# A decoder layer with expert retrieval on one core: priority for weight splits, a routing table read in pairs, up rows in longer runs

## The chip, the cores and the metric

The kernel runs on one core of a Trainium2 chip. A core has engines with an instruction queue each: TensorE (PE, matmuls; PEld is its weight load), VectorE (DVE), ScalarE (ACT), GpSimd (POOL) and SyncE (SP, which here only issues DMAs). Every engine executes its own instructions in a fixed order and waits by semaphores for the others. The metric is the time of one execution in device microseconds; lower is better.

## The reference

One layer over T = 1024 tokens of width D = 1024, all in float32: a token mixer (gated convolution plus dilated attention), then a feed-forward part that retrieves experts:

```
h = x + mixer(rms_norm(x))
u = rms_norm(h)
q = (u @ w_query).reshape(T, 8, 2, 128)        # 8 heads, two half keys
# product keys: 16 best of 128 per half, 16 best of 16*16 sums
idx, gates = ...                               # 8*16 = 128 of 16384 experts per token
a   = gelu(einsum('cd,ced->ce', u, down[idx]))
h   = h + einsum('ce,ced->cd', gates * a, up[idx])
out = rms_norm(h)
```

`down` and `up` are 16384 x 1024 each (64 MB each), and a token uses 128 rows of either.

## The kernel before

**Two ways to the experts.** Tiles of 128 tokens are treated in two ways. For tiles 0, 2 and 3 (the *side*, `experts()`) every token fetches its own rows: for each of the 128 picks POOL issues a gather of 128 rows of `down`, 512 KB (L873), DVE forms the dot product (L875), and after all of them the same with rows of `up` (L889, accumulated into `acc` on DVE, L891). That is 512 products with `down` (tile 1 takes part in these) and 384 accumulations with `up`, into four gather buffers. Tokens 512 to 1023, and the second half of tile 1's work, go through *all* experts densely, on PE.

**The dense way** has two stages. In the *hidden stage* `hidden(q)` takes four chunks of 128 experts: `weights()` (L160 to L168) loads a 512 KB chunk of `down_t`, 24 matmuls of 512 columns form its hidden values, ACT applies the gelu into `ga`. The first `STORED` = 27 of 32 groups are written to memory (`a_d`) and fetched again later; `HOLD` = 4 stay on the core; the group that is left is computed within the up stage. Beside it a builder makes the routing table `g_d` (which token uses which expert with which gate) from one-hot matrices, with matmuls (L975), copies (L977) and writes (L981). In the *up stage* each of 32 steps reads its piece of the table (`gg`, L985; `gx`, L996, for tile 1), multiplies the hidden values by it (L990) and does 120 matmuls with rows of `up` (L1063), which are summed in `held` banks, or in `psu` banks with an addition into `rest` (L1089). The last step adds the sums to `h1b` (L1093), normalizes and writes out (L855, L856).

**Float32 by halves.** Each float32 operand is split in two: `hi` is a rounding copy on ACT (L165 for weights, L181 elsewhere), `lo` the residue on DVE (L167, L182). A product then takes three matmuls, L176 (hi, hi), L177 and L178 with one `lo` each (`mm3`). For weights there are four load buffers (`RAWS`) and two pairs of `hi`/`lo` (`HILO`).

**What sets the order.** A list scheduler places the instructions of all engines by priority, which is the order in which they were written unless a block raises it. The program text interleaves the main work with the side by `yield`ed costs; the resulting order on each engine is fixed when the kernel is built. Table reads, weights and up rows share SP's queue, in issue order.

Of the kernel before, what the change touches and what calls it, by code (L numbers as in the profile page):

```python
# [8 lines left out]
F32 = mybir.dt.float32  # L9
# [4 lines left out]
ALU = mybir.AluOpType  # L14
# [3 lines left out]
P = 128  # L18
T = 1024
TH = 512  # L20
# [11 lines left out]
TC = 32  # L32
NB = 4
# [1 line left out]
PACE_D = 2.0  # L35
PACE_C = 2.2
RATE_G = 0.8
STORED = 27
HOLD = 4
RAWS = 4  # L40
HILO = 2
# [22 lines left out]

@with_exitstack
def hybrid_layer(ctx, tc, x, xT, pos, rotc, norm_mix, w_proj, w_v, conv_w, w_conv_out, w_attn_out,
                 gate_bias, w_out, norm_ffn, w_query, sub_keys, down, down_t, up, final_norm, out):
    nc = tc.nc
    V, S, G, PE = nc.vector, nc.scalar, nc.gpsimd, nc.tensor
    SIDE = getattr(nc, QUEUE)  # L70
# [90 lines left out]
    def weights(src, n=8):  # L161
        raw = wp.tile([P, n, D // n], F32, tag="raw", bufs=RAWS, name="raw")
        nc.sync.dma_start(raw, src)
        hi = wp.tile([P, n, D // n], F32R, tag="hi", bufs=HILO, name="hi")
        S.copy(hi, raw)  # L165
        lo = wp.tile([P, n, D // n], F32R, tag="lo", bufs=HILO, name="lo")
        V.tensor_tensor(lo, raw, hi.bitcast(F32), op=ALU.subtract)  # L167
        return hi, lo  # L168

    def bank(b, name):  # L170
# [729 lines left out]
    def dense():  # L900
# [47 lines left out]
        def build(srcs, c0):  # L948
# [5 lines left out]
                for c in range(c0, c0 + P // TC):  # L954
# [25 lines left out]
                    for w in range(4):  # L980
                        nc.sync.dma_start(g_d[c, :, 32 * w:32 * w + 32], stg[w])  # L981

        def weigh(q):
            gg = m8.tile([P, TH // TC, NB, TC], F32, tag="big", name="gg")
            nc.sync.dma_start(gg, g_d[:TH // TC, :, NB * q:NB * q + NB].rearrange("c j i t -> j c i t"))  # L985
            ga = gas.pop(q)
            hh, hl = bigr("hh"), bigr("hl")
            for ii in range(NB):
                v = ga[:, ii].rearrange("p (c t) -> p c t", t=TC)
                V.tensor_tensor(v, v, gg[:, :, ii], op=ALU.mult)  # L990
                split(hh[:, ii], hl[:, ii], ga[:, ii])
            parts = [(hh[:, :, tt * P:tt * P + P], hl[:, :, tt * P:tt * P + P]) for tt in range(4)]
            for k in range(len(XT)):
                gx = up_p.tile([P, P // TC, NB, TC], F32, tag="gx", bufs=GXB, name="gx")
                c0 = (TH + k * P) // TC
                nc.sync.dma_start(gx, g_d[c0:c0 + P // TC, :, NB * q:NB * q + NB].rearrange("c j i t -> j c i t"))  # L996
                xh = up_p.tile([P, NB, P], F32R, tag="xh", bufs=XHB, name="xh")
                xl = up_p.tile([P, NB, P], F32R, tag="xl", bufs=XHB, name="xl")
                view = [t.rearrange("p i (c t) -> p c i t", t=TC) for t in (xh, xl)]
                S.copy(view[0], gx)  # L1000
                V.tensor_tensor(view[1], gx, view[0].bitcast(F32), op=ALU.subtract)
                parts.append((xh, xl))
            return parts
# [30 lines left out]
        for n_q, q in enumerate(order):  # L1034
# [22 lines left out]
            for n in range(2):  # L1057
                uu = []
                whole = [bigr("uh_end"), bigr("ul_end")] if end and n else None
                for ii in range(0, NB, 2):  # L1060
                    raw = wp.tile([P, 2, TH], F32, tag="raw", bufs=RAWS, name="rawu")
                    r0 = (NB * q + ii) * P
                    nc.sync.dma_start(raw, up[r0:r0 + 2 * P, n * TH:n * TH + TH].rearrange("(a p) d -> p a d", a=2))  # L1063
                    if whole:
                        uh, ul = (t[:, ii:ii + 2] for t in whole)
                    else:
                        uh = up_p.tile([P, 2, TH], F32R, tag="uu", bufs=UPS, name="uh")
                        ul = up_p.tile([P, 2, TH], F32R, tag="uu", bufs=UPS, name="ul")
                    split(uh, ul, raw)
                    uu.append((uh, ul))  # L1070
# [105 lines left out]
```

## Time and profile before

| quantity | value |
|---|---|
| median of 3 runs | 3423.3 us (3423.22 to 3426.72) |
| profiled execution, its own time | 3433.88 us |
| its span, first to last instruction | 3432.1 us |
| PE / DVE / ACT / POOL busy | 95% / 80% / 43% / 35% of the span |
| mean granted TensorE clock | 0.984 of full speed |
| DMA | 948.08 MB in 364307 packets, 276 GB/s on average |

The span is what the rows below are cut from; 1.8 us of the profiled execution lie outside of it. Stages by the trace: mixer and query work until 1609 us (the gathers start at about 600 us), the hidden stage until 2491 us, the up stage until the end.

### The profile page before, as it was taken

The numbers are of one execution on the slowest core, as the hardware profiler recorded it, in microseconds if no ns is written. First come the engines' busy times: TensorE is split into PE (matmuls) and PEld (weight loads), VectorE is DVE, ScalarE is ACT, GpSimd is POOL, SyncE is SP. The second block draws the span as 40 slices with busy tenths as digits, with TensorE's granted clock in tenths as the row PEclk, the third lists the DMA queues.
The fourth block names the chain that finished last, engine by engine and source line by source line (L and its number), as shares of the span: only waits on it lengthen the run. The fifth ranks groups of instructions, "written<-read, shape, count | busy, mean of one in ns | idle before, by whom it ended". The sixth has DMA issues, their size and how long they took to land.

```text
span 3432.1 us, 47074 instructions
## 1 busy us (share of the span) xinstructions
PE 3274.4 (95%) x15923; PEld 2685.0 (78%) x15923; DVE 2760.1 (80%) x5646; ACT 1461.7 (43%) x3271; POOL 1190.2 (35%) x944
## 2 busy tenths in 40 slices
PE   7999999999989999988999989999999999999998
PEld 6787888887767777767777878888877878787787
DVE  4333355689999889988999999998887878888887
ACT  3544444443334353333226777787632222222222
POOL 0000000014543345555434443464544334444342
PEclk9999999999989999989999999999999999999999
DMA  4233335668888678988889898999989989999895
GB/s 129 77 119 110 103 127 191 244 230 305 302 279 276 227 260 307 342 316 292 315 316 328 329 330 334 344 340 336 348 301 336 334 316 338 326 340 333 309 350 208
DMA packets 364307, 948.08 MB, mean 276 GB/s; under 512 B 33952, under 2 KB 127648, under 8 KB 356640
## 3 DMA queue, kind: packets, MB, share of 16 engines
q1 hardware_dynamic: 232016, 465.27, 38.9%
q0 software_dynamic: 132048, 479.78, 38.8%
q8 instruction: 126, 2.06, 0.2%
q14 instruction: 117, 0.96, 0.1%
HBM read 843.15 MB, written 95.49 MB: 273 GB/s over the span
## 4 chain that ended last, share of the span: by engine, by line
PE 32%; DVE 20%; DMA 14%; issue 11%; POOL 5%; ACT 1%; SPq 0%; DVEq 0%; POOLq 0%; ACTq 0%
DVE row L875 6%; PE ps L178 6%; PE ps L176 6%; PE ps L177 6%; DMA row<-in_down,idx 5%; DMA rowu<-in_up,idx 4%; DMA gg<-g_d 4%; DVE lo L167 3%; POOL row L873 3%; POOL rowu L889 2%; PE held L177 2%; PE held L178 2%; PE held L176 2%; DVE acc L891 1%; PE psg L975 1%
## 5 line engine op out<-in xcount | busy, mean ns | idle before, releaser
L873 POOL DMA_INDIRECT row<-in_down,idx x512 | 640.9, 1252 | 885.2 <-DVE a L875 465.6
L889 POOL DMA_INDIRECT rowu<-in_up,idx x384 | 525.8, 1369 | 621.1 <-DVE acc L891 499.0
L165 ACT CAST hi<-raw 128x1024 fp32r<-128x1024 f32 x368 | 387.6, 1053 | 746.0 <-PE ps L177 541.1
L875 DVE CUSTOM_DVE_ANT_0 row<-row,ut 128x1024 f32<-128x1024 f32 x512 | 618.8, 1215 | 79.2 <-DMA row<-in_down,idx 74.0
L167 DVE TENSOR_TENSOR lo<-raw,hi 128x1024 fp32r<-128x1024 f32 x368 | 448.1, 1218 | 247.9 <-ACT hi L165 238.6
L178 PE MATMUL ps<-vhi,lo 128*128 128x512 f32 (+1 forms) x1408 | 535.4, 382 | 33.5 <-DVE lo L167 33.4
L176 PE MATMUL ps<-vhi,hi 128*128 128x512 f32 (+1 forms) x1408 | 530.6, 377 | 10.8 <-ACT hi L165 6.7
L891 DVE SCALAR_TENSOR_TENSOR acc<-rowu,a,acc 128x1024 f32<-128x1024 f32 x384 | 491.2, 1279 | 59.7 <-DMA rowu<-in_up,idx 57.3
L177 PE MATMUL ps<-vlo,hi 128*128 128x512 f32 (+1 forms) x1408 | 528.9, 376 | 0.0
L178 PE MATMUL ps<-uhi,lo 128*128 128x512 f32 x1024 | 409.1, 400 | 4.2 <-DVE lo L167 4.2
L176 PE MATMUL ps<-uhi,hi 128*128 128x512 f32 x1024 | 407.6, 399 | 5.7 <-ACT uhi L181 3.1
L177 PE MATMUL ps<-ulo,hi 128*128 128x512 f32 x1024 | 409.1, 400 | 0.5 <-DVE ulo L182 0.5
L178 PEld LDWEIGHTS ps<-vhi,lo 128*128 128x128 f32 x1408 | 269.1, 191 | 87.4 <-DVE lo L167 44.4
L176 PEld LDWEIGHTS ps<-vhi,hi 128*128 128x128 f32 x1408 | 269.7, 192 | 58.9 <-ACT hi L165 10.9
L177 PEld LDWEIGHTS ps<-vlo,hi 128*128 128x128 f32 x1408 | 269.1, 191 | 45.1
L177 PE MATMUL held<-ul,hh 128*128 128x512 f32 x624 | 247.0, 396 | 11.1 <-DVE ul L182 10.9
L178 PE MATMUL held<-uh,hl 128*128 128x512 f32 x624 | 244.0, 392 | 2.5 <-DVE hl L182 2.5
L176 PEld LDWEIGHTS ps<-uhi,hi 128*128 128x128 f32 x1024 | 194.1, 190 | 52.1 <-ACT uhi L181 5.2
L176 PE MATMUL held<-uh,hh 128*128 128x512 f32 x624 | 233.3, 393 | 0.0
L178 PEld LDWEIGHTS ps<-uhi,lo 128*128 128x128 f32 x1024 | 194.3, 190 | 47.9 <-DVE lo L167 6.4
L177 PEld LDWEIGHTS ps<-ulo,hi 128*128 128x128 f32 x1024 | 194.1, 190 | 45.1 <-issue 3.0
L181 ACT CAST hh<-ga 128x512 fp32r<-128x512 f32 x128 | 71.4, 618 | 353.0 <-DVE ga L990 348.9
(347 smaller groups left out, 5947.8 us busy)
## 6 DMA issues: line engine op xcount, KB each, us to landing
raw<-in_w_proj SPq DMA_DIRECT2D x128, 512.0 KB
raw<-in_down_t SPq DMA_DIRECT2D x128, 512.0 KB
rawu<-in_up SPq DMA_DIRECT2D x128, 512.0 KB
g_d<-stg SPq DMA_DIRECT2D x80, 512.0 KB
gg<-g_d SPq DMA_DIRECT2D x32, 1024.0 KB
a_d<-ga SPq DMA_DIRECT2D x27, 1024.0 KB
ga<-a_d SPq DMA_DIRECT2D x27, 1024.0 KB
raw<-in_w_query SPq DMA_DIRECT2D x48, 512.0 KB
```

What stands on the lines that cost most here:

```text
L165: S.copy(hi, raw)
L167: V.tensor_tensor(lo, raw, hi.bitcast(F32), op=ALU.subtract)
L176: PE.matmul(ps, l[0], r[0], start=first, stop=False)
L177: PE.matmul(ps, l[0], r[1], start=False, stop=False)
L178: PE.matmul(ps, l[1], r[0], start=False, stop=last)
L181: S.copy(hi, src)
L873: G.indirect_dma_start(out=row, out_offset=None, in_=down, in_offset=bass.IndirectOffsetOnAxis(ap=idx[:, e:e + 1], axis=0))
L875: V.tensor_tensor_reduce(out=row, in0=row, in1=ut, scale=1.0, scalar=0.0, op0=ALU.mult, op1=ALU.add, accum_out=a[:, e:e + 1])
L889: G.indirect_dma_start(out=row, out_offset=None, in_=up, in_offset=bass.IndirectOffsetOnAxis(ap=idx[:, e:e + 1], axis=0))
L891: V.scalar_tensor_tensor(acc, row, a[:, e:e + 1], acc, op0=ALU.mult, op1=ALU.add)
L975: PE.matmul(ps[:, t], ob[:, t], oa[:, t], start=True, stop=True)
```

## The change

Four edits. In `weights()` the cast and the residue are written under the scheduler's highest priority. `weigh(q)` reads the routing table for two steps in one pair of transfers: two tiles of 1 MB, each half of the tokens for eight chunks, whose runs in memory are 1 KB instead of 512 bytes, kept for both steps. It also works on half of the tokens and all four chunks at once, so the step has two products, casts and residues of 128x4x256 in place of four of 128x512. The rows of `up` come from a second copy of `up`, arranged on the host, in which one transfer's partition reads one run of 4 KB instead of two of 2 KB. `STORED` is 28, so the group that was computed within the up stage moves to the hidden stage, with one more 1 MB store and fetch.

```diff
-STORED = 27
+STORED = 28
...
         hi = wp.tile([P, n, D // n], F32R, tag="hi", bufs=HILO, name="hi")
-        S.copy(hi, raw)
         lo = wp.tile([P, n, D // n], F32R, tag="lo", bufs=HILO, name="lo")
-        V.tensor_tensor(lo, raw, hi.bitcast(F32), op=ALU.subtract)
+        with tc.high_priority():
+            S.copy(hi, raw)
+            V.tensor_tensor(lo, raw, hi.bitcast(F32), op=ALU.subtract)
...
+        pairs = {}
+
         def weigh(q):
-            gg = m8.tile([P, TH // TC, NB, TC], F32, tag="big", name="gg")
-            nc.sync.dma_start(gg, g_d[:TH // TC, :, NB * q:NB * q + NB].rearrange("c j i t -> j c i t"))
+
+            c2 = TH // TC // 2
+            if q // 2 not in pairs:
+                both = []
+                for half in range(2):
+                    gg = m8.tile([P, c2, 2 * NB, TC], F32, tag="big", name="gg")
+                    i0 = 2 * NB * (q // 2)
+                    nc.sync.dma_start(gg, g_d[c2 * half:c2 * half + c2, :, i0:i0 + 2 * NB].rearrange("c j i t -> j c i t"))
+                    both.append(gg)
+                pairs[q // 2] = both
+            gg2 = pairs[q // 2]
             ga = gas.pop(q)
             hh, hl = bigr("hh"), bigr("hl")
-            for ii in range(NB):
-                v = ga[:, ii].rearrange("p (c t) -> p c t", t=TC)
-                V.tensor_tensor(v, v, gg[:, :, ii], op=ALU.mult)
-                split(hh[:, ii], hl[:, ii], ga[:, ii])
+            for half in range(2):
+                cols = slice(half * TH // 2, half * TH // 2 + TH // 2)
+                v = ga[:, :, cols]
+                g = gg2[half][:, :, NB * (q % 2):NB * (q % 2) + NB].rearrange("p c i t -> p i c t")
+                V.tensor_tensor(v.rearrange("p i (c t) -> p i c t", t=TC), v.rearrange("p i (c t) -> p i c t", t=TC), g,
+                                op=ALU.mult)
+                split(hh[:, :, cols], hl[:, :, cols], v)
...
-                    r0 = (NB * q + ii) * P
-                    nc.sync.dma_start(raw, up[r0:r0 + 2 * P, n * TH:n * TH + TH].rearrange("(a p) d -> p a d", a=2))
+                    nc.sync.dma_start(raw, up_s[(NB * q + ii) // 2, n])
...
+        "up_s": i["peer_up"][0].reshape(P // 2, 2, P, 2, TH).transpose(0, 3, 2, 1, 4),
```

How the instructions stand now is shown at three places.

**DVE in the hidden stage**, between two weight residues (`lo`, the 262nd and 263rd of 368 by program order) while tile 1's rows of `down` are gathered (L875) and the picks of a dense tile are sorted out (L811, L814). Before:

```order
L167 TENSOR_TENSOR lo<-raw,hi 128x1024
L875 ISA row,a<-row,ut 128x1024
L875 ISA a 128x1
L811 SCALAR_TENSOR_TENSOR wq<-paf,tif 128x256
L814 TENSOR_TENSOR e_15037<-e_15037,wq 128x256
L875 ISA row,a<-row,ut 128x1024
L875 ISA a 128x1
L814 TENSOR_TENSOR other<-other,wq 128x256
L811 SCALAR_TENSOR_TENSOR wq<-paf,tif 128x256
L875 ISA row,a<-row,ut 128x1024
L875 ISA a 128x1
L167 TENSOR_TENSOR lo<-raw,hi 128x1024
```

The same place of the changed kernel:

```order
L168 TENSOR_TENSOR lo<-raw,hi 128x1024
L876 ISA row,a<-row,ut 128x1024
L876 ISA a 128x1
L815 TENSOR_TENSOR e_15037<-e_15037,wq 128x256
L815 TENSOR_TENSOR other<-other,wq 128x256
L876 ISA row,a<-row,ut 128x1024
L876 ISA a 128x1
L812 SCALAR_TENSOR_TENSOR wq<-paf,tif 128x256 x2
L876 ISA row,a<-row,ut 128x1024
L876 ISA a 128x1
L168 TENSOR_TENSOR lo<-raw,hi 128x1024
```

Three gathered rows stand between the two residues in both. Over the whole program the residues up to about the 290th stand behind the same number of gathered rows as before, within one, and behind up to ten fewer small operations; from there on the lead grows, to 13 gathered rows and some tens of smaller operations at the 319th. So the gathered rows reach the up stage later: 17 of the accumulations (L891, now L892) still stand behind the first eviction of the result.

**SP at the switch from the hidden to the up stage**: last writes of the table, up rows (`rawu`), table reads (`gg`, `gx`). Before:

```order
L981 DMA g_d<-stg 128x1024 x4
L1063 DMA rawu<-in_up 128x2x512 x2
L985 DMA gg<-g_d 128x16x128
L996 DMA gx<-g_d 128x4x128 x2
L1063 DMA rawu<-in_up 128x2x512 x4
L996 DMA gx<-g_d 128x4x128
L985 DMA gg<-g_d 128x16x128
L1063 DMA rawu<-in_up 128x2x512 x3
```

After:

```order
L982 DMA g_d<-stg 128x1024 x4
L1077 DMA rawu<-in_up_s 128x1024 x2
L1011 DMA gx<-g_d 128x4x128 x2
L994 DMA gg<-g_d 128x8x256 x2
L1077 DMA rawu<-in_up_s 128x1024 x4
L1011 DMA gx<-g_d 128x4x128
L994 DMA gg<-g_d 128x8x256 x2
L1077 DMA rawu<-in_up_s 128x1024 x4
```

The first table read now stands behind both `gx`, and two transfers of 1 MB stand where one did. On PE 128 matmuls of the hidden stage follow the last one-hot product before the first of the up stage; before there were 106.

**DVE at the end**, around the first evictions of the result (`h1b` plus `held` or `psu`). Before:

```order
L891 SCALAR_TENSOR_TENSOR acc<-rowu,a,acc 128x1024 x2
L1001 TENSOR_TENSOR xl<-gx,xh 128x4x4x32
L200 TENSOR_SCALAR st<-st 128x1
L202 RECIPROCAL st<-st 128x1
L203 TENSOR_TENSOR st<-st 128x1
L204 TENSOR_TENSOR st<-st 128x1
L205 TENSOR_SCALAR st<-st 128x1
L206 TENSOR_TENSOR st<-st 128x1
L855 SCALAR_TENSOR_TENSOR acc<-acc,st,nfin 128x1024
L1093 TENSOR_TENSOR h1b_28853<-h1b_28853,held_22593 128x512
```

After:

```order
L892 SCALAR_TENSOR_TENSOR acc<-rowu,a,acc 128x1024 x2
L1016 TENSOR_TENSOR xl<-gx,xh 128x4x4x32
L892 SCALAR_TENSOR_TENSOR acc<-rowu,a,acc 128x1024 x3
L1107 TENSOR_TENSOR h1b_28664<-h1b_28664,held_22750 128x512
L892 SCALAR_TENSOR_TENSOR acc<-rowu,a,acc 128x1024
L1107 TENSOR_TENSOR h1b_28664<-h1b_28664,psu 128x512
L1107 TENSOR_TENSOR h1b_28665<-h1b_28665,psu 128x512
L892 SCALAR_TENSOR_TENSOR acc<-rowu,a,acc 128x1024
L1107 TENSOR_TENSOR h1b_28664<-h1b_28664,held_22745 128x512
```

The gathered tiles were finished before the first eviction; now their accumulations are spread between and behind the ten evictions, with 17, 16, 16, 15, 12, 11, 10, 8, 7 and 6 still to come at each.

## Rows read from the trace of the kernel before

**Rows 1.** The page of the profile: busy time of each engine (share of the span, number of instructions), and the two large DMA queues with packets, megabytes and the time of their packets as a share of 16 engines' span. q1 carries the transfers that SP issues, q0 the gathers that POOL issues.

```profile
PE 3274.4 (95%) x15923; PEld 2685.0 (78%) x15923; DVE 2760.1 (80%) x5646; ACT 1461.7 (43%) x3271; POOL 1190.2 (35%) x944
...
q1 hardware_dynamic: 232016, 465.27, 38.9%
q0 software_dynamic: 132048, 479.78, 38.8%
```

**Rows 2.** The span cut at the stages' edges: length, busy time of PE, PEld, DVE, ACT and POOL with the number of their instructions, mean granted TensorE clock, DMA share, GB/s. 1609 to 1812 and 1812 to 2491 are the hidden stage (without and with the building of the routing table beside it), 2491 to 3423 the up stage, 2700 to 2800 a piece out of its middle.

```profile
600.00:1300.00 700.00, 663.25 (x3674) 546.50 (x3673) 621.15 (x1794) 296.95 (x579) 242.30 (x217) 0.96 0.79 267
1300.00:1609.00 309.00, 278.72 (x1257) 227.94 (x1255) 270.42 (x431) 103.94 (x194) 164.32 (x125) 0.96 0.89 317
1609.00:1812.00 203.00, 183.53 (x779) 144.64 (x778) 192.82 (x631) 60.94 (x91) 86.40 (x74) 0.99 0.88 310
1812.00:2491.00 679.00, 658.60 (x3499) 562.69 (x3499) 636.97 (x1194) 497.83 (x1559) 316.24 (x222) 0.99 0.91 337
2491.00:3423.00 932.00, 911.41 (x3936) 739.33 (x3936) 766.78 (x1015) 234.34 (x329) 378.99 (x296) 1.00 0.89 319
2700.00:2800.00 100.00, 100.00 (x438) 82.02 (x437) 83.01 (x125) 25.56 (x34) 36.44 (x30) 1.00 0.91 329
```

**Rows 3.** What PE waited for from 600 to 1300 us (columns: total us, times, longest): the two groups of waits for a weight residue. The third row is the same wait in 1300 to 1609.

```profile
PE pv L177 <- DVE lo L167: 8.3, 3, 4.0
...
PE ps L178 <- DVE lo L167: 4.9, 4, 2.2
...
PE ps L178 <- DVE lo L167: 9.1, 6, 3.6
```

**Rows 4.** The same list for 1609 to 1812.

```profile
PE ps L178 <- DVE lo L167: 12.7, 12, 2.7
PE ps L176 <- ACT hi L165: 5.2, 8, 0.9
```

**Rows 5.** The same list for 1812 to 2491.

```profile
PE ps L178 <- DVE lo L167: 9.7, 6, 1.9
PE ps L176 <- ACT hi L165: 1.4, 2, 0.9
```

**Rows 6.** The same list for 2491 to the end.

```profile
PE held L177 <- DVE ul L182: 10.9, 9, 2.4
PE ps L176 <- ACT ga L913: 3.0, 1, 3.0
PE held L178 <- DVE hl L182: 2.5, 1, 2.5
```

**Rows 7.** What DVE waited for from 2491 to the end: a piece of the routing table, and gathered rows of `up`.

```profile
DVE ga L990 <- DMA gg<-g_d: 73.3, 26, 8.4
DVE acc L891 <- DMA rowu<-in_up,idx: 32.7, 30, 4.1
```

**Rows 8.** One stall of the hidden stage in order of time (start, us, engine, line, operation, count, in brackets the idle time before it and what ended it): the cast on ACT, the residue on DVE behind a gathered row, and the matmul on PE.

```profile
1747.17 1.05 ACT L165 CAST hi<-raw 128x1024 fp32r<-128x1024 f32 x1 [3.89 <-PE ps L177]
...
1748.07 1.22 DVE L875 CUSTOM_DVE_ANT_0 row<-row,ut 128x1024 f32<-128x1024 f32 x1 [2.50 <-DMA row<-in_down,idx]
1749.22 1.22 DVE L167 TENSOR_TENSOR lo<-raw,hi 128x1024 fp32r<-128x1024 f32 x1
...
1750.49 0.50 PE L178 MATMUL ps<-vhi,lo 128*128 128x512 f32 x1 [2.68 <-DVE lo L167]
```

**Rows 9.** How long DVE stood at a residue whose cast was not done: 600 to 1300, then 1812 to 2491.

```profile
DVE lo L167 <- ACT hi L165: 36.4, 37, 5.1
DVE lo L167 <- ACT hi L165: 14.4, 11, 3.9
```

**Rows 10.** The change from the hidden to the up stage, in order of time: the last writes of the routing table and its first read as SP issues them, the first product with that read on DVE, and the first matmul of the up stage on PE.

```profile
2465.14 2.54 SPq L981 DMA_DIRECT2D g_d<-stg  x4
...
2480.21 0.37 SPq L985 DMA_DIRECT2D gg<-g_d  x1
...
2490.79 2.49 DVE L990 TENSOR_TENSOR ga<-ga,gg 128x512 f32<-128x512 f32 x4
...
2491.42 0.50 PE L176 MATMUL held<-uh,xh 128*128 128x512 f32 x1 [1.20 <-ACT xh L1000]
```

**Rows 11.** Lines of the page's groups that the change rewrites: count, busy us, mean ns of one, idle time of the engine before them.

```profile
L990 DVE TENSOR_TENSOR ga<-ga,gg 128x512 f32<-128x512 f32 x128 | 80.2, 686 | 73.3 <-DMA gg<-g_d 73.3
...
L182 DVE TENSOR_TENSOR hl<-ga,hh 128x512 fp32r<-128x512 f32 x128 | 81.2, 687 | 1.7 <-PE held L177 1.0 <-ACT hh L181 0.7
...
L182 DVE TENSOR_TENSOR ul<-rawu,uh 128x1024 fp32r<-128x1024 f32 x126 | 153.3, 1217 | 14.5 <-ACT uh L181 5.8 <-issue 4.3 <-PE psu L177 4.1
```

**Rows 12.** The end of the span on DVE: last gathered rows, last operation of the gathered tiles, first eviction of the result, last operation of all.

```profile
3395.20 2.59 DVE L891 SCALAR_TENSOR_TENSOR acc<-rowu,a,acc 128x1024 f32<-128x1024 f32 x2
...
3401.50 1.28 DVE L855 SCALAR_TENSOR_TENSOR acc<-acc,st,nfin 128x1024 f32<-128x1024 f32 x1
3402.70 0.68 DVE L1093 TENSOR_TENSOR h1b<-h1b,held 128x512 f32<-128x512 f32 x1
...
3427.58 1.42 DVE L855 SCALAR_TENSOR_TENSOR h1b<-h1b,sts,nfin 128x512 f32<-128x512 f32 x2
```

**Rows 13.** The pace of gathered rows with little else on DVE: the first and the last of four (two stand between them).

```profile
2467.08 1.29 DVE L891 SCALAR_TENSOR_TENSOR acc<-rowu,a,acc 128x1024 f32<-128x1024 f32 x1 [2.39 <-DMA rowu<-in_up,idx]
...
2475.71 1.28 DVE L891 SCALAR_TENSOR_TENSOR acc<-rowu,a,acc 128x1024 f32<-128x1024 f32 x1 [1.22 <-DMA rowu<-in_up,idx]
```

More of the change, by code (lines that the diff above doesn't have):

```diff
@@ L66, in hybrid_layer @@
 def hybrid_layer(ctx, tc, x, xT, pos, rotc, norm_mix, w_proj, w_v, conv_w, w_conv_out, w_attn_out,
-                 gate_bias, w_out, norm_ffn, w_query, sub_keys, down, down_t, up, final_norm, out):
+                 gate_bias, w_out, norm_ffn, w_query, sub_keys, down, down_t, up, up_s, final_norm, out):
     nc = tc.nc
```

## The prediction

> **What bounds the kernel now.** I read the page's busy line first: PE is busy for 3274.4 us of the 3432.1, DVE for 2760.1, and nothing else comes near [rows 1]. PE is therefore what sets the time, and a change can only win where PE stands or runs slowly; about 158 us of idle time are all there is. Next I cut the span by stages, because DVE's average of 80% hides its peaks [rows 2]. The reader should see two different regimes. In the hidden stage DVE is busy for 192.8 of 203 us and for 637.0 of 679 us, almost as tightly as PE: 10.2 and 42.0 us are left in which any of its work could be late. In the up stage it has 165 us to spare, the middle of the stage runs PE for 100.00 of 100 us, and the number of matmuls there (438 in 100 us) gives 0.228 us for each. Then I asked what PE waited for in each stage. In the hidden stage it is nearly always a weight residue, `lo`, or its cast, `hi` [rows 4, 5]; in the up stage it is the split of up rows and of the weighted hidden values [rows 6]. Last I followed one stall and the end of the span on DVE [rows 8, 12].
>
> The stall shows the mechanism that the change's first edit aims at. The cast was done at about 1748.2. DVE stood for a gathered row (2.50 us), did its product, began the residue at 1749.22, and PE, which had needed it for 2.68 us, went on at 1750.49. So PE's waits are not for DVE's throughput alone: a residue stands in line behind a product whose data come late.
>
> I make the sum on the profiled execution, 3433.9 us with its span of 3432.1. The median of the runs shown is 3423.3, so I carry the differences over to that.
>
> **The change, part by part.**
>
> *Priority of cast and residue.* The two instructions remain the same, 368 each; only their place changes, and it can change only by what stands ahead of them. The rows of the order tell two cases. Up to about the 290th residue the same gathered rows stand ahead, and a few small operations fewer; at the place shown, three rows before and three after. There a late row still blocks the residue. From there to the end of the hidden stage up to 13 rows fewer stand ahead.
> - Up to 1609 us: the waits shown are 8.3, 4.9 and 9.1 us, 22.3 together [rows 3]. With the same rows ahead I take 3 us off. Bounds: 0 and 22.
> - 1609 to 1812: 12.7 + 5.2 = 17.9 us of waits, and a granted clock of 0.99, worth about 2 us over 203 [rows 2, 4]. A few small operations of some 0.4 us leave the way, rows stay. I take 8, a little under half. Bounds: 0 and 20.
> - 1812 to 2491: 9.7 + 1.4 = 11.1 us, and 0.01 of clock over 679 us, 7 us [rows 2, 5]. Here rows do leave the way, so I take all of the waits and none of the clock: 11. Bounds: 0 and 18.
>
> A cast that goes first on ACT costs nothing by itself: ACT had stood for 3.89 us before the one shown, until PE released the `hi` buffer [rows 8]. The cost is on DVE: a residue put at the head of the line before its cast is done makes the rows behind it wait. I price that as a rival.
>
> *What is put off is late at the end.* Thirteen rows (1.28 us each, [rows 12]) and some tens of small operations, about 35 us of DVE's work, move out of the hidden stage. In the up stage DVE has room, but the order is fixed, and 17 accumulations still stand behind the first eviction, where there were none. Before, the first eviction ran at 3402.70, behind the gathered tiles' own end (last accumulations at 3395.20, normalized by 3402.7), and the last operation ended at 3429.0, 3.1 us before the end of the span. Now DVE has from about 3400 on: 17 accumulations at 1.25 us, 21; ten evictions at 0.6, five normalizations of 1.4 and their small steps of 0.16, 19; the gathered tiles' end, 5. That is 45 us, so 3445, and 3448 with the 3.1 us of output, against 3432: **+15**, a part of the small steps lying in the rows' waits. If the rows came at the pace at which they came with little else on DVE, (2475.71 - 2467.08) / 3 = 2.88 us [rows 13], 17 of them are 49 us and the end is at 3457: +25. As weights and up rows are no longer streamed at that point, I take the first. Lower bound: +13, if the first eviction starts two us earlier.
>
> *Table read for two steps.* Half as many transfers carry the same bytes in runs twice as long. Of the 73.3 us for which DVE stood at `gg` [rows 7] that takes nothing by the runs' length as such, but the order now issues both halves four to eight up rows ahead of the product, and the second step's products have no read right ahead of them. On DVE a pair of 0.686 us products and of residues becomes one operation of 128x1024; by the up rows' residue, 1.217 us against 2 x 0.687 [rows 11], that saves 0.156 us for each of 128 pairs, 20 us, off the path since DVE has 165 us to spare. On the path are the 10.9 us that PE stood for `ul` and 2.5 for `hl` [rows 6], splits that stood behind such a product.
>
> *The group moved to the hidden stage.* Its 96 matmuls, 22 us, run in either place; it takes the wait of 3.0 us in [rows 6] out of the up stage. The extra store and fetch are 2 MB of 948, hidden as the other 27 are. With the last item I take 16 of the 16.4 us. Bounds: 0 and 20 (the smaller waits too).
>
> *Up rows in 4 KB runs.* The two queues are the evidence: 465.27 MB in 232016 packets, 2.0 KB each, take 38.9% of the engines' span, 479.78 MB in 132048 packets, 3.6 KB each, 38.8% [rows 1]. That is 0.0836% and 0.0809% of the span per megabyte, 3% apart. The 128 transfers are 67 MB, 5.6% of 3432 or 192 us of all 16 engines, and 3% of that is 6 us, spread over the 932 us of the stage. PE's waits [rows 6] name the splits of up rows, not the loads, so I take 0. Bounds: 0 and -6. The Trainium skill's page "Perfetto Trace Analysis", in the section on DMA optimizations, speaks the other way: it says that going from 2 KB to 4 or 8 KB can dramatically improve throughput. The trace does not agree: its two queues, at 2.0 and 3.6 KB a packet, cost the same within those 3%. Were the page right here, the gathered rows would also come sooner, which is the rival "much faster".
>
> *The switch.* Before, the first read of the table was issued 2480.21 - 2465.14 = 15.1 us after the last writes, was there at 2490.79, 10.6 us on, and the first matmul of the up stage ran 0.6 us later, 1.20 us late [rows 10]. Now two reads are needed: 15.1 + 2 x 10.6 = 36.3 us. PE has 128 matmuls to do meanwhile, 29.2 us, where it had 106. **+7**. Bounds: -1 (the first half suffices for the first products) and +12 (both `gx`, too, go first).
>
> **Sum:** -3 - 8 - 11 - 16 + 15 + 7 = -16, from 3432 to 3416 on the profile and from 3423.3 to **3407** on the median.
>
> **Rivals.**
> *No difference.* If a residue is late only by the rows ahead of it, the first two terms fall to 0 and the sum to -5, 3418; with the tail at 2.88 us a row as well it is +5, 3428. For it: the place shown in the order has the same rows. Against it: from the 290th on the order does differ, and the up stage's term doesn't hang on it.
>
> *Slower: residues wait for their casts at the head of DVE's line.* DVE has stood there already: 36.4 us in 37 places from 600 to 1300, 14.4 us in 11 from 1812 to 2491, and not once in 1609 to 1812 [rows 9]. If each of the 128 chunks of the hidden stage now stands for 0.4 us, well under the 1.0 us of the 37 places, that is 51 us, as much as DVE's whole slack there (52 us); rows slip by as much and lie in front of the evictions. With a third of it hidden in waits for rows, +35: about 3442. It decides from 16 / 128 = 0.13 us a chunk if nothing is hidden. Against it: `hi` was done a microsecond ahead of its residue's turn in [rows 8], and the position of the residues has barely moved for most of the stage.
>
> *Much faster.* All waits named above go (22.3 + 20 + 18 + 20) and only the switch and the tail stay (+22): -58, about 3365. It asks that rows be early too, which is what lighter transfers would do. Against it: 0.88 to 0.91 of the DMA share in all stages concerned [rows 2], and bytes are unchanged.
>
> **How the numbers follow.** The forecast, 3392 to 3418, has 0.45 (its ends: the tail at +25 makes the sum -6; the casts' three terms at 38 instead of 22, half of the way to their bounds or a little less, make it -32); no difference, 3418 to 3430, 0.19; slower, about 3442, 0.22; much faster, about 3365, 0.14. A tenth of a per cent is the spread of the three runs, so 0.2%, 6.8 us, is what I call a difference: faster 0.59 (forecast and much faster), same 0.19, slower 0.22. The range goes to 3370 and 3440: it leaves out the lower half of the fast case and the upper half of the slow one, 0.18 together.
>
> **What would show it.** Right: DVE's wait for `gg` under 20 us; PE's wait for `ul` near 0; PE's wait for `lo` from 1609 on at most half of the 22.4 us; a gap on PE of some 7 us at the first matmul of the up stage; accumulations between the evictions, and an end about 45 us after the first of them. Wrong: DVE standing at `lo` for its cast for more than 30 us from 1609 on (the slower case), a residue wait on PE as before (no difference), or a first eviction that is early by more than 40 us (much faster).

## The result, and the profile after

The changed kernel takes 3401.6 us (median of 5 runs, 3392.4 to 3402.8) where the kernel before, run beside it, takes 3426.7. The ratio is 0.9922 with a 95% interval of 0.9902 to 0.9942: 0.8% faster, which is 27 us by the ratio and 25 by the two medians. I had forecast 16 us. The profiled execution has a span of 3401.1 us against 3432.1, 31 us less.

The page of the changed kernel, busy times and the two large queues, answers to [rows 1]:

```profile
PE 3265.4 (96%) x15923; PEld 2683.8 (79%) x15923; DVE 2750.0 (81%) x5518; ACT 1462.5 (43%) x3207; POOL 1232.4 (36%) x944
...
q0 software_dynamic: 132048, 479.78, 39.6%
q1 hardware_dynamic: 183152, 467.37, 38.4%
```

DVE lost 10 us of work, not the 20 that I had counted for the wider operations. I had counted with the mean length of one operation, but neighbours overlap: 128 products of 0.686 us kept DVE busy for 80.2 us [rows 11], not 87.8. SP's queue carries nearly the same bytes in a fifth fewer packets for a cost per megabyte only 2.6% lower (38.4% of 3401.1 us for 467.37 MB; 38.9% of 3432.1 for 465.27).

To see where the time went I cut each trace at four instructions of PE, which all kernels here have: the starts of the last matmul of the query keys, the last of the hidden stage, the first and the last of the up stage. The group of 96 matmuls that moved is counted in the hidden stage everywhere, at 0.227 us each (21.8 us). All times in microseconds, each from one profiled execution, and some of these lie off their kernel's median: before 3433.9 against 3426.7, before + moved group 3422.1 against 3410.7, with 6 gather buffers 3412.8 against 3422.7.

```
kernel                          hidden stage   gap to up stage   up stage   last matmul to end
before                              895.9            1.6           909.1           9.7
changed                             870.8            0.3           881.6          32.0
changed, no priority                895.3            0.2           880.5           9.8
changed, no paired read             878.7            1.2           892.9          33.0
changed, plain up rows              880.5            1.4           880.7          30.5
before + priority                   876.5           15.9           914.1          12.0
before + moved group                898.3            0.2           899.7          10.7
before + up rows in 4 KB            894.2            1.9           903.5           9.8
changed, 5 split buffers            873.6            0.9           948.7           9.6
changed, 17 rows left out           875.4            0.7           880.7           9.7
changed, priority on 21 chunks      885.0            0.2           880.8          34.0
changed, 6 gather buffers           881.2            0.2           889.7           9.8
the same, no priority               940.7            0.2           888.9           9.8
changed, 40 gate products on ACT    874.3            7.3           884.4          10.5
```

The first two rows are the result: -25 in the hidden stage, -1 at the switch, -28 in the up stage, +22 at the end, -31 in all. What lies ahead ended at 1615.8 and 1616.5 us. With the priority it ended between 1610.6 and 1616.5 in seven kernels, without it in the mixers between 1604.9 and 1615.8 in five (the two with 6 gather buffers aside), so the mixers gave nothing that shows; one kernel with no instruction moved was 6.6 us early. So a single span says little below some 10 us, and the medians and stages have to be read together. The hidden stage varies as much: in five kernels with one and the same order on DVE there (changed, no paired read, plain up rows, 5 split buffers, 17 rows left out) it took 870.8 to 880.5 us, 875.8 on average, and the changed kernel's is the shortest of them. In the four without the priority and with 4 gather buffers it took 894.2 to 898.3.

**Hidden stage.** PE's waits from its start to its end, 1616 to 2488, in the changed kernel (total us, times, longest):

```profile
PE ps L179 <- DVE lo L168: 11.5, 14, 2.0
PE ps L177 <- ACT hi L167: 2.8, 6, 0.5
```

That is 14.3 us where [rows 4, 5], from 1609 on, had 29.0, so the waits for residues and casts were halved. But they were not halved evenly. The stage in four pieces, first before, then changed (length, busy time of PE, PEld, DVE, ACT, POOL, granted clock, DMA share, GB/s):

```profile
1616.00:1812.00 196.00, 177.76 (x751) 139.76 (x749) 185.82 (x616) 60.10 (x86) 81.28 (x71) 0.99 0.88 311
1812.00:1930.00 118.00, 115.25 (x618) 98.60 (x619) 115.79 (x245) 86.30 (x274) 50.21 (x39) 1.00 0.93 339
1930.00:2050.00 120.00, 109.14 (x573) 93.29 (x572) 118.94 (x333) 88.63 (x281) 48.65 (x38) 0.94 0.88 319
2050.00:2490.00 440.00, 433.99 (x2311) 370.79 (x2310) 401.24 (x617) 322.16 (x1006) 216.69 (x144) 1.00 0.92 341
```

```profile
1616.00:1812.00 196.00, 182.27 (x768) 142.89 (x766) 187.41 (x615) 61.55 (x87) 82.50 (x72) 0.98 0.88 316
1812.00:1930.00 118.00, 114.39 (x604) 96.80 (x603) 112.72 (x227) 81.26 (x255) 51.34 (x41) 1.00 0.90 329
1930.00:2050.00 120.00, 119.25 (x647) 102.23 (x646) 120.00 (x345) 95.41 (x299) 45.81 (x35) 1.00 0.90 332
2050.00:2488.00 438.00, 436.58 (x2341) 374.37 (x2340) 401.31 (x627) 326.77 (x1014) 206.47 (x140) 1.00 0.92 342
```

The third row is the one. Before, DVE was full for 120 us on end, PE stood for 11 us and ran at a granted clock of 0.94 on average: 13.6 of the 120 us at 0.5, the lower of its two levels (1.2 GHz), and of that the longest piece, 6.8 us from 1988.1 on, began while PE stood for 5.9 us. After, DVE is just as full, but PE runs 119.25 of 120 us at 1.00, 647 instructions instead of 573. In terms of residues it is twelve of them: the 291st began 4.9 us earlier than before, counted from the query stage's end, the 303rd 29.1 us earlier, and the 363rd 32.7.

What left the way between these residues can be read from DVE's work there, 110.9 us from the 291st to the 303rd before and 86.7 after, full in both. Before, products with gathered rows and, of the table's building, the `oa` operations, from 1939 to 2051 (line, count, busy us, mean ns, idle time before them):

```profile
L875 DVE CUSTOM_DVE_ANT_0 row<-row,ut 128x1024 f32<-128x1024 f32 x36 | 43.5, 1212 | 1.1 <-DMA row<-in_down,idx 1.1
L962 DVE TENSOR_TENSOR oa<-iota,sT 128x512 f32<-128x512 f32 x28 | 18.7, 680 | 0.0
```

After, from 1935 to 2023:

```profile
L876 DVE CUSTOM_DVE_ANT_0 row<-row,ut 128x1024 f32<-128x1024 f32 x26 | 31.2, 1207 | 0.0
L963 DVE TENSOR_TENSOR oa<-iota,sT 128x512 f32<-128x512 f32 x20 | 12.9, 675 | 0.0
```

Between the two residues ten gathered rows fewer (12 us) stand in line, and 16 operations of the table's building fewer (`oa` and `ob`, 11 us). That is nearly the 24.2 us gained there. The lead does not grow much behind it: 11 gathered rows fewer stand ahead of the 303rd residue, and 11 ahead of the 319th, where I had counted 13.

**Switch.** SP, DVE and PE of the changed kernel at the switch (start, us, engine, line, operation, idle time before):

```profile
2474.28 3.84 SPq L994 DMA_DIRECT2D gg<-g_d  x2
...
2485.16 2.36 DVE L1004 TENSOR_TENSOR ga<-ga,gg 128x1024 f32<-128x1024 f32 x2 [1.81 <-DMA gg<-g_d]
2487.56 1.23 DVE L183 TENSOR_TENSOR hl<-ga,hh 128x1024 fp32r<-128x1024 f32 x1
2490.22 2.36 DVE L1004 TENSOR_TENSOR ga<-ga,gg 128x1024 f32<-128x1024 f32 x2 [1.43 <-DMA gg<-g_d]
...
2487.58 0.50 PE L177 MATMUL held<-uh,hh 128*128 128x512 f32 x1
```

The second half of the table was there 5 us behind the first, and PE began before it was there.

**Up stage.** DVE's largest wait for the table there, and all that PE waited for from the switch to the end:

```profile
DVE ga L1004 <- DMA gg<-g_d: 22.9, 13, 3.6
...
PE held L178 <- DVE ul L183: 0.8, 1, 0.8
```

73.3 us became 22.9, and PE's waits of [rows 6] are gone. 3840 matmuls at 0.228 us are 875.5; the stage takes 881.6.

**End.** DVE and POOL, which answers to [rows 12], and ahead of them all accumulations from 3350 on in one row (count, duration, first and last start):

```profile
L892 DVE SCALAR_TENSOR_TENSOR acc<-rowu,a,acc x18: 1265/1283/1319, 3349.3 to 3384.8; 128x1024 f32<-128x1024 f32 x18
...
3350.50 0.68 DVE L1107 TENSOR_TENSOR h1b<-h1b,held 128x512 f32<-128x512 f32 x1
...
3384.78 1.28 DVE L892 SCALAR_TENSOR_TENSOR acc<-rowu,a,acc 128x1024 f32<-128x1024 f32 x1 [1.06 <-DMA rowu<-in_up,idx]
...
3391.11 1.28 DVE L856 SCALAR_TENSOR_TENSOR acc<-acc,st,nfin 128x1024 f32<-128x1024 f32 x1
3392.68 0.57 POOL L857 DMA_DIRECT2D out<-acc  x1 [12.56 <-DVE acc L856]
```

PE is done at 3369; what follows is DVE's work, the rows that were put off among it, and the last gathered tile's 512 KB of output, issued at 3392.68.

### The profile page after: what moved, and what is told of

It reads as the page before. It is cut to its first block, busy times and chain, and to the rows that moved or that the text cites. A ratio compares the mean times of both kernels' runs of the same rounds, so it can differ in the third digit from the quotient of the medians.

```text
span 3401.1 us, 46840 instructions
## 1 busy us (share of the span) xinstructions
PE 3265.4 (96%) x15923; PEld 2683.8 (79%) x15923; DVE 2750.0 (81%) x5518; ACT 1462.5 (43%) x3207; POOL 1232.4 (36%) x944
## 3 DMA queue, kind: packets, MB, share of 16 engines
q1 hardware_dynamic: 183152, 467.37, 38.4%
## 4 chain that ended last, share of the span: by engine, by line
PE 35%; DVE 11%; DMA 7%; issue 5%; POOL 2%; ACT 0%; POOLq 0%; SPq 0%; DVEq 0%; ACTq 0%
PE held L178 4%; PE held L179 4%; PE held L177 4%; PE ps L179 4%; PE ps L178 3%; PE ps L177 3%; DVE row L876 3%; DMA row<-in_down,idx 3%; PE psu L178 3%; PE psu L177 3%; PE psu L179 3%; PE psg L976 3%; DMA rowu<-in_up,idx 2%; DVE lo L168 2%; DMA g_d<-stg 1%
## 5 line engine op out<-in xcount | busy, mean ns | idle before, releaser
L874 POOL DMA_INDIRECT row<-in_down,idx x512 | 658.0, 1285 | 853.1 <-DVE a L876 463.6
L890 POOL DMA_INDIRECT rowu<-in_up,idx x384 | 550.7, 1434 | 594.5 <-DVE acc L892 457.0
L892 DVE SCALAR_TENSOR_TENSOR acc<-rowu,a,acc 128x1024 f32<-128x1024 f32 x384 | 491.1, 1279 | 51.9 <-DMA rowu<-in_up,idx 49.5
```

What stands on the lines that cost most here:

```text
L874: G.indirect_dma_start(out=row, out_offset=None, in_=down, in_offset=bass.IndirectOffsetOnAxis(ap=idx[:, e:e + 1], axis=0))
L890: G.indirect_dma_start(out=row, out_offset=None, in_=up, in_offset=bass.IndirectOffsetOnAxis(ap=idx[:, e:e + 1], axis=0))
L892: V.scalar_tensor_tensor(acc, row, a[:, e:e + 1], acc, op0=ALU.mult, op1=ALU.add)
```

## The experiments

Two questions: which edit bought which stage, and whether the 22 us at the end are the price of the priority. Times are medians; ratios are against the kernel before, run beside it.

**Without the priority.**

```diff
-        with tc.high_priority():
-            S.copy(hi, raw)
-            V.tensor_tensor(lo, raw, hi.bitcast(F32), op=ALU.subtract)
+        S.copy(hi, raw)
+        V.tensor_tensor(lo, raw, hi.bitcast(F32), op=ALU.subtract)
```

> The changed kernel with the casts and residues back at their ordinary priority; the other three edits stay. My theory: the 25 us that the hidden stage lost came from the priority, so PE's waits for residues return there (+20 to +25); but only 4 accumulations instead of 17 now stand behind the first eviction, which gives back 14 to 16 of the 22 us at the end. Together +5 to +11 over the changed kernel's 3401.6: 3407 to 3413. Rival (the hidden stage was shortened by something else, such as the moved group or the lighter reads): the hidden stage stays at 871 us, the tail still shrinks, about 3386.

Measured: 3396.7 us, 0.9901 (0.9879 to 0.9922), below my range and no slower than the changed kernel. The hidden stage went back to 895.3 as my theory had it, but the tail fell by all of its 22 us: the four rows that were left fitted between the evictions. By these two traces the priority gains 24.5 us and costs 22.2; by the five kernels with the changed kernel's order it gains some 20. PE's waits in the hidden stage without it:

```profile
PE ps L178 <- DVE lo L167: 14.0, 14, 2.3
PE psg L975 <- ACT stg L977: 13.9, 6, 6.7
PE ps L176 <- ACT hi L165: 6.2, 9, 0.9
```

The second row is no weight residue: the table's one-hot matmuls wait for copies on ACT. The copies themselves had stood, in part, for the table's writes to leave their buffers (`stg`), 30.9 us in this stage:

```profile
L977 ACT COPY stg<-psg 128x128 f32<-128x128 f32 x640 | 126.3, 286 | 68.6 <-PE psg L975 32.8 <-DMA g_d<-stg 30.9 <-issue 3.4
```

In the changed kernel that is 19.6 us, and PE's wait for these copies 1.9. How the priority brings this about is not shown.

**The priority alone**, in the kernel before, with the same three lines.

> The kernel before with the priority of casts and residues alone. My theory: PE's waits for residues and casts in the hidden stage fall by half as in the changed kernel, -20 to -25 there, and with one accumulation left at the first eviction the end costs 0 to 3: 3402 to 3408 against 3426.7 before. Rival (priority changes nothing by itself): 3423 to 3428. Rival (residues at the head of the line hold up the rows): above 3430.

Measured: 3433.4 us, 1.0006 (0.9990 to 1.0022): no difference, and my range missed. The hidden stage did gain 19.4 us. Most of it was given back at once, in one wait of PE at the switch (the gap grew by 14.3 us), the rest in the up stage (5.0) and at the end (2.3):

```profile
PE held L177 <- ACT xh L1001: 15.5, 1, 15.5
```

The hidden stage's matmuls are the cover under which the last piece of the table is written and read back ([rows 10]: 26.3 us from the last writes to the first matmul of the up stage). Run earlier, they are no longer there to cover it: 32 matmuls followed the last one-hot product before the first of the up stage, where there had been 106, and from the last writes to that first matmul it still took 22.5 us. In the changed kernel the moved group's 96 matmuls, 22 us, are that cover: 128 = 32 + 96.

**Priority on 21 chunks only**, those around the crowded 120 us.

```diff
+    calls = [0]
+
     def weights(src, n=8):
+        calls[0] += 1
...
-        with tc.high_priority():
+        with tc.high_priority() if 286 <= calls[0] <= 306 else ExitStack():
             S.copy(hi, raw)
```

> The changed kernel with the priority on 21 of the 368 weight chunks only, the 286th to the 306th, where the runs so far put the whole difference between the hidden stage with priority (871 us) and without (895 us). 20 accumulations stand behind the first eviction. My theory: the priority pays only where DVE is full for 110 us on end, so these 21 chunks give the hidden stage its 20 to 25 us, and the rows they put off cost the end 22 to 26 us: 3398 to 3408, no better than without any priority (3396.7). Rival (the gain comes from all chunks, in small pieces): the hidden stage at 888 us or more, and 3415 to 3425.

Measured: 3410.4 us, 0.9953 (0.9937 to 0.9969), just above my range and slower than without any priority (0.9901, intervals apart). The place is confirmed: the 303rd residue is 23.2 us ahead of before, with 21 of 368 chunks preferred. But by the 315th only 6.5 us were left and by the 363rd 14.6, where the changed kernel had 32.7; the stage kept 10 of the 20 to 25 that I had expected, and 20 rows still stood at the end (34.0). So the later chunks' priority holds the gain, it does not make it.

**The tail priced.**

```diff
-            for e in range(P):
+            for e in range(P - 17 if tt == 3 else P):
```

> The changed kernel without the last 17 gathered rows of up of the last gathered tile, the ones that stood behind the first eviction; their part of that tile's result is left out. This prices the tail. My theory: the end moves to about 10 us behind PE's last matmul, as before the change, -22: 3378 to 3382. Rival (the evictions and the output set the tail, the rows lie in their waits): -5 or less, 3396 to 3402.

Measured: 3379.4 us, 0.9860 (0.9837 to 0.9882), 22.3 us less behind the last matmul (9.7 instead of 32.0); the other stages moved by less than 5 us. The rows are the tail.

**Without the paired read.** `weigh(q)` as before the change, one read of 1 MB per step in 512 byte runs and four products.

> The changed kernel with the routing table read again for one step at a time, in runs of 512 bytes, and four products per step; the other three edits stay, and the same 17 accumulations are left at the first eviction. My theory: the up stage's 28 us are due to the paired read. DVE stands at the table's read again for some 70 us instead of 24.7, PE waits for the splits of up rows again, 11 to 20 us: 3413 to 3422. Rival (the moved group freed the up stage): at most +5, 3402 to 3407.

Measured: 3415.9 us, 0.9962 (0.9946 to 0.9978): 0.4%, 14 us, slower than the changed kernel. DVE stands at the table for 72.1 us again, and the up stage takes 11.3 us more, so this edit brought 11 of its 28 us and not all, as I had thought (7.9 us more were spent in the hidden stage, whose order on DVE is the same):

```profile
DVE ga L991 <- DMA gg<-g_d: 72.1, 24, 7.2
...
PE held L178 <- DVE ul L183: 5.9, 2, 3.4
PE psu L177 <- DVE rest L1089: 4.5, 5, 1.3
```

The run undoes the reads in pairs and the wider products together; which of the two frees PE is not shown.

**The moved group alone**, `STORED = 28` in the kernel before.

> The kernel before with the 28th group moved from the up stage to the hidden stage, alone. My theory: the up stage loses its wait of 3.0 us for that group and its few disturbed splits, and 4 accumulations are left at the first eviction, which cost 3 to 5 us: 3422 to 3430 against 3426.7, no difference that can be told. Rival (the moved group is what freed the up stage, 28 us): 3395 to 3405.

Measured: 3410.7 us, 0.9953 (0.9935 to 0.9972). My theory, no difference, is wrong by 16 us; the rival, all of the 28 us, is wrong too. The up stage lost 9.4 us, three times the 3.0 us that its listed wait was worth, and the four rows left at the end cost 1. As the profiled execution is 11 us slower than the median, the stages do not show where the rest of the 16 us lies.

**The up rows' runs**, undone in the changed kernel and alone in the kernel before.

```diff
-                    nc.sync.dma_start(raw, up_s[(NB * q + ii) // 2, n])
+                    r0 = (NB * q + ii) * P
+                    nc.sync.dma_start(raw, up[r0:r0 + 2 * P, n * TH:n * TH + TH].rearrange("(a p) d -> p a d", a=2))
```

> The changed kernel with the up rows read from the plain table in runs of 2 KB again; the other three edits stay and the order of instructions is the same. My theory: transfers of up rows are off the path, 3398 to 3406 (no difference). Rival (longer runs lighten the DMA engines, so gathered rows come sooner, and that is what cleared the up stage): +10 to +25, 3412 to 3427, with longer waits of DVE for gathered rows.

> The kernel before with the up rows in 4 KB runs, alone; no instruction changes its place. My theory: 3420 to 3428, no difference. Rival (lighter transfers): 3400 to 3415, with shorter waits of DVE for the table and for gathered rows.

Measured: undone 3403.1 us, 0.9917 (0.9895 to 0.9940), which is the changed kernel's ratio; alone 3421.1 us, 0.9980 (0.9967 to 0.9993). So with the paired read they are worth nothing that shows (880.7 against 881.6 in the up stage), and without it 5.6 us in the up stage, though DVE's wait for the table is not shorter there (77.7 us in the run alone). A fifth of a per cent is at the edge of what these runs resolve. Undone, DVE stands at the table for 41.4 us instead of 22.9, and PE does not feel it; DVE's waits for gathered rows are no longer than in the changed kernel (38.7 us in all against 41.1), so the rival is out:

```profile
DVE ga L1004 <- DMA gg<-g_d: 41.4, 18, 4.6
```

**Can the tail be had back?** Fewer buffers for the splits of up rows, `UPS = 5` instead of 7, let the scheduler put all rows ahead of the evictions.

> The changed kernel with 5 instead of 7 buffers for the splits of up rows. The scheduler then puts the splits later and all accumulations ahead of the first eviction. My theory: the tail falls from 32 us behind PE's last matmul to about 10, -22; with fewer splits ready ahead, PE waits for some of them, +5 to +25: 3385 to 3405. Rival (the gathered rows cannot come faster than they do, so what the tail gives PE's waits take, and more): 3405 to 3425.

Measured: 3445.6 us, 1.0060 (1.0043 to 1.0076), above both my range and the rival's. The tail is 9.6, but the up stage went from 881.6 to 948.7, with PE waiting for additions and splits that now stand behind up to 35 more rows:

```profile
PE psu L177 <- DVE rest L1103: 29.2, 16, 3.1
PE held L177 <- ACT uh L182: 9.4, 8, 1.2
PE held L178 <- DVE ul L183: 6.0, 11, 2.7
```

More gathers in flight, `ROWS = 6` and `BIGS = 9`, with the priority and without:

> The changed kernel with 6 gather buffers instead of 4 and 9 big buffers instead of 10 (8 KB per partition for 8 KB). The scheduler then runs the gathered rows 44 to 52 ahead through the hidden stage, and none is left at the first eviction. My theory (the tail is rows put off, and they can be done earlier if more gathers are in flight): the tail falls to 10 us, the hidden stage takes up to 15 us more, since the rows are done there and before: 3375 to 3395. Rival (DVE is full from 600 us on, so rows done earlier push residues back by as much): 3395 to 3410. Rival (a ninth big buffer fewer stalls the table's reads): above 3410, with PE gaps in the up stage.

> As the run with 6 gather and 9 big buffers, but casts and residues at ordinary priority. My theory: the rows run further ahead still (659 instead of 638 at the last weight residue) at the hidden stage's expense, so the priority is worth something here: 3385 to 3405, 5 to 25 us behind the run with priority. Rival (the priority is worth nothing once the tail is gone either way): within 5 us of it.

Measured: 3422.7 us, 0.9973 (0.9956 to 0.9989), and 3470.0, 1.0120 (1.0096 to 1.0145), both well above my ranges. The tail is 9.8 in both. With the priority the hidden stage took 10 us more than in the changed kernel, the up stage 8 more, and 14 were lost ahead of them (the query keys ended at 1630.0). Which of the two buffer counts cost the up stage its 8 us was not tried. Without the priority the rows were 76 further ahead than before by the 290th residue, the 291st came 68 us later than before, and the stage took 940.7 us. This is the clearest row on what the priority does: it chooses whether DVE's work ahead of a fixed point is residues or rows, and with more rows at hand the choice is worth 60 us in the hidden stage, 47 in the medians.

**Less work for DVE instead of another order.** 40 of the 160 products with the gates in the table's building go to ACT:

```diff
-                            V.tensor_tensor(ob, ob, gv[:, :, None].to_broadcast([P, 4, P]), op=ALU.mult)
+                            if t4 % 4 == 0:
+                                for t in range(4):
+                                    S.mul(ob[:, t], ob[:, t], gv[:, t:t + 1])
+                            else:
+                                V.tensor_tensor(ob, ob, gv[:, :, None].to_broadcast([P, 4, P]), op=ALU.mult)
```

> The changed kernel, priority included, with 40 of the 160 gate products of the table's building moved from DVE (0.6 us each, 24 us) to ACT (four products of 0.32 us each, 52 us; ACT is busy for 565 of 895 us in the hidden stage). 4 accumulations instead of 17 are left at the first eviction, 600 gathered rows instead of 594 are done at the last weight residue. My theory: the priority only puts DVE's work off, and what it puts off is paid at the end; with 24 us of DVE's work gone the hidden stage keeps its 871 us and the tail falls from 32 to 12 to 16 us: 3380 to 3390. Rival (rows come no faster, and ACT, in order, now holds up the table's building): PE waits for the table's copies and casts, the hidden stage at 880 us or more, 3390 to 3405. It is also the try at a kernel that beats both.

Measured: 3385.7 us, 0.9886 (0.9863 to 0.9909), the fastest kernel here with the whole computation. The hidden stage kept 874.3 us and the tail fell to 10.5. Against the changed kernel's 0.9922 that is 12 us, with intervals that just overlap; against 0.9901 without the priority they overlap widely, so it beats the kernel before surely, the changed one probably. The moved products on ACT and the crowded 120 us of this kernel:

```profile
L971 ACT ACTIVATE ob<-ob,sT 128x128 f32<-128x128 f32 x160 | 51.7, 407 | 0.6
...
1930.00:2050.00 120.00, 118.77 (x635) 100.91 (x634) 115.82 (x316) 99.63 (x311) 45.84 (x37) 1.00 0.90 329
```

PE runs as in the changed kernel, with 4 us of room on DVE. It waits 6.9 us for a cast at the switch, where only 33 matmuls follow the last one-hot product, so not all of the 21.5 us at the end is kept.

## Why the prediction was right, and where its steps were not

The time, 3401.6, lies in the range and near the forecast of 3407, in the likeliest case's band of 3392 to 3418. The terms behind it did worse than their sum: against the spans, where I had -16 and -31 was measured, they underrated the gain by some 26 us (hidden stage, up stage, switch) and overrated it by 11 (ahead of 1609, end), which partly cancelled. That the median came within 6 us is in part luck.

**Up to 1609, -3:** 0. The stage ended 0.7 us later, and a term of 3 us is below what single spans can show.

**1609 to 2491, -8 and -11:** measured -25 together (-20 by the five kernels of one order), in another division. Up to the 291st residue, where the same rows stand ahead, it was 4.9 us; the rest came where rows leave the way, as I had argued, but in 12 chunks, and half of what left there was the table's building. I took the waits listed from 1812 on, 11.1 us, as all there was to get, and left the clock out. The idle time and the slow matmuls of the crowded 120 us alone are more than that: 10.9 us idle, and 13.6 us at half clock, worth 6.8. The step that failed is the use of PE's wait list for weights where the table's matmuls waited as well: from 1812 to 2491 they held 8.5 of the 19.6 us that the list named, so that "nearly always a weight residue" was a misreading.

**Up stage, -16:** -27.5. The same error, larger. I summed the waits by name, 16.4 us. The stage's own length would have said it: 930.9 us, less 21.8 for the moved group and 875.5 for 3840 matmuls, is 33.6 us of loss, where the whole list, small waits included, came to 20.7. Read along the experiments it splits into the moved group (-9.4), the priority and the longer runs together (-6.8, from 899.7 to 892.9), and the paired read (-11.3). The signs that I had named came, nearly: DVE's wait for the table fell to 22.9 (I had said under 20), PE's for `ul` to 0.8. But the first of them is no measure of the gain, as it is 41.4 with the plain up rows and PE as fast.

**Switch, +7:** -1. I had added two transfers of 10.6 us one behind the other and counted PE's start from the second. The second landed 5 us behind the first, and the first half was enough to begin with; that was the bound of -1, and I chose the wrong end.

**End, +15:** +22.3. DVE's part was right: from the first eviction to the last operation's start 3391.11 - 3350.50 = 40.6 us, where I had 45. But the first eviction came 18.6 us before PE's last matmul and not 22 (my rounding: before the change it was 19.7), and the last gathered tile, now last of all, took 8.4 us from its output's issue to the end of the span (3392.68 to 3401.1), where I had kept 3.1 from a smaller one.

**Priority as a whole.** My sum gave it -22 in the stages and +15 at the end. The two traces give -24.5 and +22.2 (-20 over the five kernels): with it and without it the kernel is the same within the measurement. That it costs about what it gains was not among my rivals. The slower rival did not come: DVE stood for casts for 12.3 us from 1616 to 2488, where it had 14.4 [rows 9]. Nor did the much faster one. The up rows' runs, which I took at 0, are 0 in the changed kernel; the Trainium skill's "Perfetto Trace Analysis", section on DMA optimizations, says that batching small transfers into larger ones, as from 2 KB to 4 or 8 KB, can dramatically improve throughput. Here each transfer stays at 512 KB and only its runs grow from 2 to 4 KB, and the best ratio is 0.9980.

What stays open: which part of the -6.8 us between 899.7 and 892.9 in the up stage is due to the runs and which to the priority, and why the moved group alone frees 9.4 us. Both are of the size by which single spans differ, though the up stage alone varied less where PE hardly waits in it (880.5 to 881.6 us in five kernels with the paired read and the moved group). The paired read was not run without the moved group.

## What to carry to other kernels

Take a stage's loss from its length less its count of matmuls times their pace, not from the list of waits: here the list held half of it. A priority on a full engine takes no work off it; it decides which work is late. So look up where the displaced work comes due and what it covered before (here the last 22 us, or a wait of 15.5 us at the next switch): in the changed kernel that ate the gain, with 6 gather buffers, where nothing came due at the end, the priority was worth 47 us. Taking work off the engine as well gave the fastest kernel here. Two edits that each leave the end nearly untouched can fill it together: one and four rows were left over by the priority and the moved group alone, 17 by both (with the paired read or without it).

## What the runs showed of the hardware that I had not expected

The tail's gathered rows came at 2.1 us each (18 between 3349.3 and 3384.8), with evictions between them, and DVE stood for them for only 4.3 us of that time, where such rows came every 2.88 us before the switch [rows 13]. The DMA engines' share was 0.84 there (3349 to 3385) and 1.00 before the switch (2467 to 2477). And the two 1 MB reads of the table, issued within 3.84 us, were there 10.9 and 15.9 us after the first's issue (2474.28 to 2485.16 and 2490.22), where a single one had taken 10.6 [rows 10]. (Reads of `gx`, 256 KB each, were issued just ahead of the two, and just behind the single one.) Here a transfer's time was no price that adds up over two.
